# Up-projections of a two-layer encoder: half the row tiles by a 2x2 scheme of seven products

## The chip, the cores and the metric

The kernel runs on one core of a Trainium2 chip. The metric is device time in microseconds: the time of one execution, taken as the median of several runs. TensorE (PE in the profile) multiplies matrices from SBUF into PSUM, VectorE (DVE) and ScalarE (ACT) do elementwise work on both memories, GpSimd (POOL) does little here, and SyncE (SP) issues most transfers from HBM. Each engine works through its own queue in order; semaphores make one wait for another.

## The reference

256 tokens of width 2048 pass two layers, one with attention and pooling, one with an mLSTM. Both layers end in the same gated MLP, the part that matters here:

```
def conv_ffn(x, w_up, conv_w, conv_b, w_down):
    u = x @ w_up
    up = jnp.pad(u, ((0, 0), (1, 1), (0, 0)))
    c = conv_w.astype(u.dtype)
    u = c[0] * up[:, :-2] + c[1] * up[:, 1:-1] + c[2] * up[:, 2:] + conv_b.astype(u.dtype)
    gate, val = jnp.split(u, 2, axis=-1)
    return (jax.nn.silu(gate) * val) @ w_down
```

`w_up` is 2048 x 11264 (gate and value, 5632 columns each), `w_down` 5632 x 2048, everything float32. `x` has gone through an RMS norm before, and the result is added to the residual.

## The kernel before

**Precision.** Each float32 operand is split into a high part in a shorter matmul format (float32r) and a low part, the rest. A product is then three matmuls: high by high, high by low, low by high. Activations are split once (`norm.xx`, 16 K tiles x {high, low} x 256 tokens). Weights are split as they stream in.

**The stream of weights.** `Stream` holds one list of weight chunks of 128 x 1024 float32 (512 KB) in the order in which TensorE uses them. `load` issues a chunk's transfer on SP into a raw buffer `w` (six of them); `split` makes the high part on ScalarE (L89) and the low part on VectorE (L90) in a buffer `hl` (four). `next` hands TensorE its chunk and first tops up both, five chunks loaded ahead and two split ahead. The hosts' part (`_up_chunks`, `_down_chunks`, `_ffn_order`) only lays the weights out in that order.

**The MLP.** The 44 row tiles of the hidden width (128 gate rows and 128 value rows each) are done in chunks of 4, 8, 8, 8, 8 and 8 (`FCH`). For each chunk, `up` makes its row tiles, and then `down` adds the previous chunk's share to the residual, 512 output columns at a time (four groups); the last chunk's `down` ends the layer.

- `up` (L886) runs `stat_group`: 16 K tiles, weights stationary, tokens moving. Per K tile there are two matmuls 512 columns wide (the weights' high part by both parts of the activations) and two 256 wide (low part by high). The result lies in PSUM with hidden rows on partitions. `gather` (L365 to L368) adds its two halves with a ScalarE copy and a VectorE add, L890 multiplies by the norm's scale `R` per token, L894 to L897 are the convolution over tokens, L900 to L903 the gate and the split of the result into `g`.
- `down` (L933) runs `mov_part`: activations stationary, 512 weight columns moving, six matmuls per K tile, then two VectorE adds into `x` (`residual`, L376).

**PSUM.** Both kinds of group use tag `mm`, two buffers of two banks each: one is filled while the other is read. The remaining four banks are the tag `ps`, for transposes and small products.

**Order.** TensorE's order is the program's order (a manual schedule). The other engines' queues are ordered by the compiler's scheduler. `Weave` keeps small side tasks (norms, attention heads) that TensorE takes in between: `wv.tick(dt)` advances a nominal clock after each few matmuls, and a task is continued when its delay has passed.

Of the kernel before, what the change touches and what calls it, by code (L numbers as in the profile page):

```python
# [9 lines left out]
F32 = mybir.dt.float32  # L10
# [6 lines left out]
P = 128  # L17
# [47 lines left out]
class Stream:  # L65


    def __init__(self, nc, wpool, spool, srcs, load_ahead, split_ahead):
        self.nc, self.wpool, self.spool, self.srcs = nc, wpool, spool, srcs
        self.la, self.sa = load_ahead, split_ahead  # L70
        self.w, self.hl = {}, {}
        self.n_load = self.n_split = self.at = 0

    def load(self, pieces=1):
        i = self.n_load
        width = self.srcs[i].shape[-1]
        n = width // pieces
        w = self.wpool.tile([P, CH * P], F32, tag="w", name=f"w{i}")
        for c in range(0, width, n):
            self.nc.sync.dma_start(w[:, c : c + n], self.srcs[i][:, c : c + n])  # L80
        self.w[i] = w, n, width
        self.n_load += 1

    def split(self, then=None):
        i = self.n_split
        w, n, width = self.w.pop(i)
        hl = self.spool.tile([P, 2, CH * P], F32R, tag="hl", name=f"hl{i}")
        for c in range(0, width, n):
            (self.nc.vector.tensor_copy if i + c == 0 else self.nc.scalar.copy)(hl[:, 0, c : c + n], w[:, c : c + n])  # L89
            self.nc.vector.tensor_sub(hl[:, 1, c : c + n], w[:, c : c + n], hl[:, 0, c : c + n].bitcast(F32))  # L90
            then and then(c // n)
        self.hl[i] = hl
        self.n_split += 1
# [63 lines left out]
def trunk(ctx: ExitStack, tc: tile.TileContext, gx, xT, xn, call, catt, cml, weights, out):  # L157
# [212 lines left out]
    def bc(ap, n):  # L370
        return ap.unsqueeze(1).to_broadcast([ap.shape[0], n, ap.shape[1]])
# [500 lines left out]
    def ffn_layer(layer, norm, nxt):  # L872
        with ExitStack() as es:
            def lp(name, bufs):
                return es.enter_context(tc.tile_pool(name=name, bufs=bufs, reuse_waits="tile"))

            tp = lp(f"ff{layer}", 2)

            def cw(tl, j):
# [5 lines left out]

            def up(f, gt, i):  # L886
                ps = stat_group(xx, list(range(KT)), f"up{layer}_{f}")
                wv.until(lambda: norm.R is not None)
                u = gather(tp, ps, f"up{layer}_{f}")
                v.tensor_mul(u, u, bc(norm.R, 2))  # L890
                y = tp.tile([P, 2, S], F32, tag="y", name=f"y{layer}_{f}")
                for j in range(2):
                    tl = f + j * FT
                    a.activation(y[:, j, :], u[:, j, :], AF.Identity, scale=cw(tl, 1), bias=cw(tl, 3))  # L894
                    v.scalar_tensor_tensor(y[:, j, 1:S], u[:, j, 0 : S - 1], cw(tl, 0), y[:, j, 1:S],  # L895
                                           ALU.mult, ALU.add)
                    v.scalar_tensor_tensor(y[:, j, 0 : S - 1], u[:, j, 1:S], cw(tl, 2), y[:, j, 0 : S - 1],  # L897
                                           ALU.mult, ALU.add)
                s_ = tp.tile([P, S], F32, tag="silu", name=f"s{layer}_{f}")
                a.activation(s_, y[:, 0, :], AF.Silu)  # L900
                v.tensor_mul(s_, s_, y[:, 1, :])
                a.copy(gt[:, i, 0, :], s_)
                v.tensor_sub(gt[:, i, 1, :], s_, gt[:, i, 0, :].bitcast(F32))  # L903

            def down_end(gt, b, kts):
# [26 lines left out]

            def down(c, gt, last):  # L933
                kts = list(range(FCH[c]))
                for b in range(NB):
                    if last and nxt is None and b == NB - 1:
                        down_end(gt, b, kts)
                        break
                    ps = mmp.tile([P, 2, 512], F32, tag="mm", name=f"dn{layer}_{c}_{b}")
                    mov_part(ps, lambda k: gt[:, k], kts, True, True)  # L940
                    residual(ps, b)
                    if last and nxt is None:
                        nc.sync.dma_start(out[:, :, b * 512 : b * 512 + 512], x[:, :, b * 512 : b * 512 + 512])
                    elif last:
                        nxt.add(b)

            wv.add(norm.finish(), 4.0)
            f, gts = 0, []
            for c, n in enumerate(FCH):
                gt = actp.tile([P, 8, 2, S], F32R, tag=f"B{c % 2}", name=f"g{layer}_{c}")  # L950
                gts.append(gt)
                for i in range(n):
                    up(f, gt, i)
                    f += 1
                if c:
                    down(c - 1, gts[c - 1], False)
            down(len(FCH) - 1, gts[-1], True)

# [68 lines left out]

def _ffn_order():

    seq, u, d = [], 0, 0  # L1030
    for c, n in enumerate(FCH):
        seq += [("u", u + i) for i in range(4 * n)]
        u += 4 * n
        if c:
            m = FCH[c - 1] // 4 * 8
            seq += [("d", d + i) for i in range(m)]
            d += m
    m = FCH[-1] // 4 * 8
    seq += [("d", d + i) for i in range(m)]
    return seq  # L1040
# [100 lines left out]
```

## Time and profile before

| | before |
|---|---|
| median of 3 runs | 2205.43 us (2205.32 to 2205.55) |
| span of the profiled execution | 2203.1 us |
| granted TensorE clock | 1.000 |
| bytes read from HBM | 411.58 MB, 188 GB/s over the span |

The profiled execution's span runs from the first to the last instruction; the time of a run also holds the start and the end around it. In the page, a group of instructions shows its line, engine, operation, output and inputs by the program's names, shapes and count, then busy time, the mean of one in ns, and the idle time of the engine just in front with what ended most of it. Matmuls are pipelined, so the sum of single durations is more than the time they take; the chain that ended last (the work followed back from the last instruction) gives pieces that add up to the span.

### The profile page before, as it was taken

To read this page: it belongs to the slowest core of one execution; us is meant where nothing else is said; L and a number is where in the kernel's file an instruction comes from. 1 tells how busy PE (TensorE), PEld (TensorE's weight loads), DVE (VectorE), ACT (ScalarE), POOL (GpSimd) and SP (SyncE) were. 2 spreads that over 40 slices of the span, in tenths; PEclk is the share of its full clock that TensorE was granted. 3 is DMA by queue.
4 is the path that set the end of the run, shared out by engine and by line. 5 is a ranking of instruction groups with operands and counts; after the bars stand their busy time and mean duration, and the time that the engine had idled before them with its cause. 6 is when DMAs were issued, how large, how long until landed. Compare 5 with 4: busy or idle time off the path is not lost.

```text
span 2203.1 us, 30458 instructions
## 1 busy us (share of the span) xinstructions
PE 2197.9 (100%) x11616; PEld 1883.7 (86%) x11616; DVE 1525.5 (69%) x2172; ACT 1169.0 (53%) x1664; POOL 28.1 (1%) x40
## 2 busy tenths in 40 slices
PE   9999999999999999999999999999999999999999
PEld 8888888888888888889888888888888888888887
DVE  7686677776776767666767676667777677676764
ACT  7665555554554545456555454555555455454542
POOL 0020000000000000000000000000000000000000
PEclk9999999999999999999999999999999999999999
DMA  9555556556565666656565555556555656555664
GB/s 323 179 164 170 175 191 187 190 189 198 184 194 188 192 191 191 196 171 205 162 202 177 185 181 171 186 177 191 186 191 189 197 185 193 189 191 191 192 191 144
DMA packets 118036, 415.71 MB, mean 189 GB/s; under 512 B 13082, under 2 KB 15426, under 8 KB 117890
## 3 DMA queue, kind: packets, MB, share of 16 engines
q1 hardware_dynamic: 114656, 409.76, 58.2%
q10 hardware_dynamic: 3074, 3.75, 0.6%
q8 instruction: 91, 1.49, 0.3%
q14 instruction: 55, 0.45, 0.1%
q0 software_dynamic: 160, 0.26, 0.0%
HBM read 411.58 MB, written 2.14 MB: 188 GB/s over the span
## 4 chain that ended last, share of the span: by engine, by line
PE 100%; DVE 0%; issue 0%
PE up L203 45%; PE dn L203 21%; PE op L203 8%; PE mv L203 4%; PE mq L203 4%; PE mk L203 4%; PE mo L203 4%; PE qproj L203 3%; PE pool L203 1%; PE kproj L203 1%; PE vproj L203 1%; PE qk L203 1%; PE av L203 1%; PE end L203 0%; PE xt L254 0%; PE sc L203 0%
## 5 line engine op out<-in xcount | busy, mean ns | idle before, releaser
L90 DVE TENSOR_TENSOR hl<-w,hl 128x1024 fp32r<-128x1024 f32 (+2 forms) x772 | 939.1, 1218 | 466.6 <-ACT hl L89 464.8
L89 ACT CAST hl<-w 128x1024 fp32r<-128x1024 f32 (+1 forms) x771 | 806.9, 1047 | 677.3 <-PE dn L203 242.1
L203 PE MATMUL up<-xx,hl 128*128 128x512 f32 (+1 forms) x5632 | 984.2, 337 | 0.0
L203 PEld LDWEIGHTS up<-xx,hl 128*128 128x128 f32 x5632 | 857.9, 188 | 125.9
L203 PE MATMUL dn<-hl,g 128*128 128x512 f32 x2064 | 471.3, 389 | 0.0
L203 PEld LDWEIGHTS dn<-hl,g 128*128 128x128 f32 x2064 | 386.2, 188 | 79.5
L366 ACT COPY tb_up<-up 128x512 f32<-128x512 f32 x88 | 51.7, 587 | 154.0 <-PE up L203 154.0
L367 DVE TENSOR_TENSOR tb_up<-up,tb_up 128x512 f32<-128x512 f32 x88 | 60.8, 691 | 97.0 <-ACT tb_up L366 97.0
L894 ACT ACTIVATE y<-tb_up,cst 128x256 f32<-128x256 f32 x176 | 96.4, 595 | 47.0 <-DVE tb_up L890 47.0
L203 PE MATMUL mk<-xx,hl 128*128 128x512 f32 (+1 forms) x512 | 92.2, 337 | 0.0
L203 PE MATMUL mq<-xx,hl 128*128 128x512 f32 (+1 forms) x512 | 92.1, 337 | 0.0
L203 PE MATMUL mv<-hl,xx 128*128 128x512 f32 (+2 forms) x480 | 91.7, 350 | 0.0
L203 PE MATMUL op<-hl,cat 128*128 128x512 f32 x384 | 91.6, 393 | 0.0
L203 PE MATMUL mo<-hl,xx 128*128 128x512 f32 x384 | 90.4, 391 | 0.0
L203 PE MATMUL op<-hl,mcat 128*128 128x512 f32 x384 | 89.5, 392 | 0.0
L203 PEld LDWEIGHTS mq<-xx,hl 128*128 128x128 f32 x512 | 79.2, 188 | 11.6
L203 PEld LDWEIGHTS mk<-xx,hl 128*128 128x128 f32 x512 | 79.0, 188 | 11.4
L203 PEld LDWEIGHTS mv<-hl,xx 128*128 128x128 f32 x480 | 78.3, 189 | 11.2
L203 PEld LDWEIGHTS op<-hl,mcat 128*128 128x128 f32 x384 | 71.5, 188 | 14.6
L203 PEld LDWEIGHTS mo<-hl,xx 128*128 128x128 f32 x384 | 71.0, 188 | 14.2
L203 PEld LDWEIGHTS op<-hl,cat 128*128 128x128 f32 x384 | 70.9, 188 | 14.1
L895 DVE SCALAR_TENSOR_TENSOR y<-tb_up,cst,y 128x255 f32<-128x255 f32 x176 | 76.8, 478 | 0.0
(209 smaller groups left out, 1270.4 us busy)
## 6 DMA issues: line engine op xcount, KB each, us to landing
w<-in_up SPq DMA_DIRECT2D x352, 512.0 KB, 3.6
w<-in_dn SPq DMA_DIRECT2D x176, 512.0 KB, 4.1
w<-in_m_in SPq DMA_DIRECT2D x124, 512.0 KB, 4.1
w<-in_a_in SPq DMA_DIRECT2D x46, 512.0 KB, 4.4
w<-in_a_out SPq DMA_DIRECT2D x32, 512.0 KB, 3.4
w<-in_m_out SPq DMA_DIRECT2D x32, 512.0 KB, 3.5
w<-in_m_g SPq DMA_DIRECT2D x5, 432.0 KB, 3.4
x<-in_xn SPq DMA_DIRECT2D x4, 512.0 KB, 9.5
```

What stands on the lines that cost most here:

```text
L89: (self.nc.vector.tensor_copy if i + c == 0 else self.nc.scalar.copy)(hl[:, 0, c : c + n], w[:, c : c + n])
L90: self.nc.vector.tensor_sub(hl[:, 1, c : c + n], w[:, c : c + n], hl[:, 0, c : c + n].bitcast(F32))
L203: pe.matmul(out_, lhsT, rhs, start=start, stop=stop, skip_group_check=True)
L366: a.copy(tb, ps[:, :, 1, :])
L367: v.tensor_add(tb, ps[:, :, 0, :], tb)
L894: a.activation(y[:, j, :], u[:, j, :], AF.Identity, scale=cw(tl, 1), bias=cw(tl, 3))
L895: v.scalar_tensor_tensor(y[:, j, 1:S], u[:, j, 0 : S - 1], cw(tl, 0), y[:, j, 1:S], ALU.mult, ALU.add)
```

## The change

In each layer's chunks 2 to 6, the last four of the eight row tiles are no longer made by `up` but by `quads`, one "quad" per chunk. The first four, and all of the first chunk, stay as they are.

**The scheme.** A quad's product is (256 tokens x 2048) by (2048 x 1024). The tokens are cut in two blocks of 128, K in pairs of 128, the columns in two halves of 512. Seven block products, in Winograd's form of Strassen's scheme, take the place of eight. Each product has tokens stationary, 512 columns moving, and three matmuls per K pair. The operands are blocks or sums of blocks:

- sums of activations (`sums`, four of them, `sx`) are made once per layer on VectorE and split by ScalarE and VectorE; they use a buffer of the next chunk's `g` as scratch;
- sums of weights (four blocks, two per chunk): the stream's chunk 2 of each K pair is loaded as two copies of block 12, then chunk 1's content (blocks 11 and 22) is added to it by a second, accumulating transfer on GpSimd's queue; chunk 3 (blocks 22 and 21) has two VectorE adds before its split. So a K pair takes three chunks, and four more chunks per quad carry block 21 for the seventh product: 28 chunks where four row tiles took 16.

**PSUM.** Products 1 and 3 accumulate over the whole quad in one `mm` buffer, products 5, 7, 6, 4 in the four `ps` banks. The 28 quad steps (six matmuls each) are spread between the slots of the other groups by `_ffn_plan`: `up` and `down` are generators now and yield between chunks. The first quad starts with chunk 2's first slot, the next three at slot 8 of 32, the last from slot 6 to 24, with the block-21 steps behind.

**After the products.** `decode` combines the seven with six VectorE and some ScalarE operations and applies the norm's scale per token (a partition here). `finish` transposes the results on TensorE (four 128 x 128 per row tile), copies them out, and goes on in `tail`, the old end of `up`.

**Buffers.** In the MLP the stream has seven raw and five split buffers, seven loads and three splits ahead; `tail` writes the gate over `y` and has no buffer of its own for it.

The core of the diff:

```diff
     def load(self, pieces=1):
         i = self.n_load
-        width = self.srcs[i].shape[-1]
+        src = self.srcs[i]
+        kind, src, plus = src if isinstance(src, tuple) else ("plain", src, None)
+        width = src.shape[-1]
...
+        if plus is not None:
+            self.nc.gpsimd.dma_start(w[:, :width], plus, accum_op=ALU.add)
...
+        if kind == "one":
+            self.one = w
+        if kind == "two":
+            self.nc.vector.tensor_add(w[:, 0:512], w[:, 0:512], self.one[:, 0:512])
+            self.nc.vector.tensor_add(w[:, 512:1024], w[:, 512:1024], w[:, 0:512])
...
+            def sums():
+                vv = actp.tile([P, 2, KT // 2, S], F32, tag="B1", name=f"v{layer}")
+                for h in range(2):
+                    ks = slice(8 * h, 8 * h + 8)
+                    v.tensor_add(vv[:, 0], norm.xx[:, ks, 0, :].bitcast(F32), norm.xx[:, ks, 1, :].bitcast(F32))
...
+                    v.tensor_sub(s1, a21, a22)
+                    v.tensor_add(s3, a11, a21)
+                    yield 3.0
+                    v.scalar_tensor_tensor(s2, s1, -1.0, a11, ALU.mult, ALU.subtract)
+                    v.tensor_sub(s4, s3, a12)
+                    v.tensor_sub(s4, s4, a22)
...
+                    for j in range(4):
+                        hi, lo = (sx[:, j, 4 * h : 4 * h + 4, i, :] for i in range(2))
+                        a.copy(hi, raw[:, j])
+                        v.tensor_sub(lo, raw[:, j], hi.bitcast(F32))
+                        yield 2.0
...
+            def product(bank, act, w, c, first, last):
+                (xh, xl), (wh, wl) = act, (w[:, j, c : c + 512] for j in range(2))
+                mm(bank, xh, wh, first, False)
+                mm(bank, xh, wl, False, False)
+                mm(bank, xl, wh, False, last)
+                wv.tick(0.68)
...
+            def quads(fs, gt, i0, name):
+                banks = {}
+                m = KT // 2
+                for p in range(m):
+                    ends = p == 0, p == m - 1
+                    for k in range(3):
+                        hl = st.next()
...
+                        left = ((1, block_of(2 * p, 0)), (3, sum_of(3, p))), \
+                            ((5, sum_of(0, p)), (7, sum_of(2, p))), ((6, sum_of(1, p)), (4, block_of(2 * p + 1, 1)))
+                        for n, (j, act) in enumerate(left[k]):
+                            product(banks[j], act, hl, n * 512, *ends)
+                        if p == m - 1 and k == 0:
+                            c12 = cp1.tile([P, 512], F32, tag="c12", name=f"c12_{name}")
+                            a.copy(c12, banks[1])
+                        if p == m - 1 and k == 2:
+                            c12, c21, c22 = decode(banks, c12, name)
+                            wv.add(finish(c12, c22, fs[2:], gt, i0 + 2, name), 7.0)
+                        yield
+                for p in range(0, m, 2):
+                    hl = st.next()
+                    for n in range(2):
+                        product(banks[1], block_of(2 * (p + n) + 1, 0), hl, n * 512, False, p + n == m - 1)
+                    if p == m - 2:
+                        c11 = cp1.tile([P, 512], F32, tag="c11", name=f"c11_{name}")
+                        a.activation(c11, banks[1], AF.Copy, scale=norm.rcol[:, 0:1])
+                        wv.add(finish(c11, c21, fs[:2], gt, i0, name), 4.0)
+                    yield
+            def decode(banks, c12, name):
...
+                v.tensor_add(c12, c12, banks[6])
+                v.tensor_add(c21, c12, banks[7])
+                a.activation(c21, c21, AF.Copy, scale=r1)
+                a.activation(c12, c12, AF.Copy, scale=n0)
+                v.scalar_tensor_tensor(c12, banks[3], n0, c12, ALU.mult, ALU.add)
+                v.scalar_tensor_tensor(c12, banks[5], n0, c12, ALU.mult, ALU.add)
+                v.scalar_tensor_tensor(c22, banks[5], r1, c21, ALU.mult, ALU.add)
+                v.scalar_tensor_tensor(c21, banks[4], r1, c21, ALU.mult, ALU.subtract)
+                return c12, c21, c22
+            def finish(top, bottom, fs, gt, i0, name):
+                for n, f in enumerate(fs):
+                    tr = psp.tile([P, 2, S], F32, tag="ps", name=f"tr{layer}_{f}")
+                    for j in range(2):
+                        for t, src in enumerate((top, bottom)):
+                            c = (2 * j + n) * P
+                            pe.transpose(tr[:, j, t * P : t * P + P], src[:, c : c + P], ident)
+                    u = tp.tile([P, 2, S], F32, tag="tb", name=f"tb_{layer}_{f}")
+                    a.copy(u, tr)
+                    tail(u, f, gt, i0 + n)
+                    yield 2.5
...
+            wv.add(sums_ready(), 8.0)
+            st.la, st.sa, st.more = 7, 3, (lp(f"fw{layer}", 1), lp(f"fh{layer}", 1), st.at + len(_ffn_plan()))
...
+def _ffn_plan():
+    plan = []
     for c, n in enumerate(FCH):
+        whole = n - 4 if c else n
+        fill = [("n", c, i) for i in range(whole)]
+        if c:
+            down = [("d", c - 1, b) for b in range(NB)]
+            fill = fill[:2] + down[:1] + fill[2:3] + down[1:2] + fill[3:] + down[2:]
+        slots = []
+        for e in fill:
+            slots += [e] * (4 if e[0] == "n" else FCH[e[1]] // 2)
...
+        if c > 1:
+            for k in range(4):
+                here[k + 1].append(("s", c - 1, 0))
+        first, end = (0, len(slots)) if c == 1 else (8, len(slots)) if not late else (6, 24)
+        for k in range(3 * m):
+            here[first + k * (end - first) // (3 * m)].append(("s", c, 0))
+        if late:
+            for k in range(4):
+                here[end + k].append(("s", c, 0))
+        for e, extra in zip(slots, here):
+            plan += [e] + extra
```

In a plan, "n" is one chunk of an up group, "d" one of a down group, "s" one quad step.

More of the change, by code (lines that the diff above doesn't have):

```diff
@@ L959, in trunk @@
+            for e in run.values():
+                assert next(e, None) is None
+            st.la, st.sa, st.more = 5, 2, None
     norms = [Norm(0), None]
```

165 lines of the change are left out of this document (120 added, 45 removed).

## The prediction

> **What bounds the kernel now.** I read the page's head and chain first, to see which engine ends the program.
>
> ```profile
> span 2203.1 us, 30458 instructions
> PE 2197.9 (100%) x11616; PEld 1883.7 (86%) x11616; DVE 1525.5 (69%) x2172; ACT 1169.0 (53%) x1664; POOL 28.1 (1%) x40
> ...
> PE 100%; DVE 0%; issue 0%
> ```
>
> TensorE never waits: 100% of the span and of the chain. Matmuls taken off it shorten the program as long as everything else keeps its cover; DVE at 69% is the nearest cover. Busy times of single matmuls overlap, so I take their price from the chain in order of time, where the pieces add up.
>
> ```profile
> 256.15 3.48 PE up L203 x20
> 260.06 0.71 PE up L203 x4
> ...
> 413.01 89.16 PE up L203 x512
> 502.18 43.53 PE dn L203 x192
> ```
>
> Eight up-projection tiles (64 matmuls each, half of them 512 and half 256 columns wide) take 89.16 us, 11.145 us a tile. A down-projection matmul (512 columns, a new stationary block each time) takes 43.53/192 = 0.2267 us. Between the first two pieces lies 260.06 − 256.15 − 3.48 = 0.43 us, and this piece of the timeline fills it:
>
> ```profile
> 259.46 0.60 PE L254 MATMUL xt<-cst,x 128*128 128x128 f32 x4
> ```
>
> four transposes, 0.1075 us each on the path.
>
> **The matmuls removed and added.** A "quad" is four row tiles of one chunk (1024 columns of the weights, gate and value). Before: 4 × 11.145 = 44.58 us. After: seven products × eight K pairs × three matmuls = 168, all 512 wide with a new stationary block each, the form of the down row: 168 × 0.2267 = 38.09 us. That is −6.49 us, and with five quads a layer and two layers −64.9 us. The results come out with tokens on partitions, so `finish` transposes them back, 16 per quad, 160 × 0.1075 = +17.2 us. On TensorE alone: −47.7 us.
>
> **The wait that the change can add.** The `mm` tag has two buffers, and a group's end is read while the next group fills the other. During a quad products 1 and 3 hold one (`two`), so consecutive up and down groups share the other. What lies between is one quad step of six matmuls, 6 × 0.2267 = 1.36 us. The reading takes this long now:
>
> ```profile
> 634.71 2.67 PE L203 MATMUL dn<-hl,g 128*128 128x512 f32 x11
> 634.91 0.59 ACT L366 COPY tb_up<-up 128x512 f32<-128x512 f32 x1 [1.74 <-PE up L203]
> ...
> 635.53 0.69 DVE L367 TENSOR_TENSOR tb_up<-up,tb_up 128x512 f32<-128x512 f32 x1 [1.10 <-ACT tb_up L366]
> ```
> ```profile
> 678.24 2.01 PE L203 MATMUL up<-xx,hl 128*128 128x512 f32 x10
> ...
> 678.44 1.29 DVE L376 TENSOR_TENSOR x<-x,dn 128x512 f32<-128x512 f32 x2 [0.41 <-PE dn L203]
> ```
>
> From the switch to the next group until the buffer is read: 635.53 + 0.69 − 634.71 = 1.51 us for an up group, 678.44 + 1.29 − 678.24 = 1.49 us for a down group. The gap from one to the next instruction in these rows (635.53 − 634.91 − 0.59) is 0.03 us, so the buffer is free at about 1.55 us, 0.19 us after the six matmuls end. In the plan I count 36 such ends a layer (9 around the second chunk's quad, 7 in each of the next three, 6 in the last), 72 in all. At the lower bound, ScalarE and VectorE both idle as in these rows (1.74, 1.10 and 0.41 us of idleness in front), 72 × 0.19 = 13.7 us. At the upper bound a whole split has just begun ahead of the eviction: 0.19 + 1.22 (the split's row, below), 101 us. I take 0.35 us, nearer to the lower end: VectorE will seldom be idle (next part), but the splits run up to three chunks ahead of TensorE, and their order is laid out in advance so that evictions can come first. That is +25 us. What queues behind a TensorE that waits is everything: its order is written by hand.
>
> By the Trainium skill, "Perfetto Trace Analysis", section Matmuls, independent groups should rotate through different PSUM banks so that an eviction overlaps the next group's matmuls; that rule speaks against giving one of the two buffers away. Taken alone it would charge the whole 1.55 us at each end, 112 us, and 2205.4 − 47.7 + 112 = 2270 us. The rows speak for less, because the quad steps in between write other banks and are that overlap; no run so far shows it.
>
> **VectorE's load.** A steady pair of an up chunk and a down chunk, by its groups and its window:
>
> ```profile
> L90 DVE TENSOR_TENSOR hl<-w,hl 128x1024 fp32r<-128x1024 f32 x48 | 58.6, 1222 | 30.8 <-ACT hl L89 30.8
> L89 ACT CAST hl<-w 128x1024 fp32r<-128x1024 f32 x48 | 50.4, 1050 | 43.7 <-PE dn L203 23.6 <-PE up L203 20.1
> ...
> L895 DVE SCALAR_TENSOR_TENSOR y<-tb_up,cst,y 128x255 f32<-128x255 f32 x16 | 7.0, 478 | 0.0
> L897 DVE SCALAR_TENSOR_TENSOR y<-tb_up,cst,y 128x255 f32<-128x255 f32 x16 | 7.0, 477 | 0.0
> L890 DVE TENSOR_TENSOR tb_up<-tb_up,R 128x512 f32<-128x512 f32 x8 | 5.5, 692 | 0.3
> L367 DVE TENSOR_TENSOR tb_up<-up,tb_up 128x512 f32<-128x512 f32 x8 | 5.5, 691 | 8.8 <-ACT tb_up L366 8.8
> ```
> ```profile
> L376 DVE TENSOR_TENSOR x<-x,dn 128x512 f32<-128x512 f32 x94 | 60.4, 684 | 18.6 <-PE dn L203 18.6
> ...
> L903 DVE TENSOR_TENSOR g<-s,g 128x256 fp32r<-128x256 f32 x88 | 36.8, 419 | 0.0
> L901 DVE TENSOR_TENSOR s<-s,y 128x256 f32<-128x256 f32 x88 | 36.8, 418 | 0.6 <-ACT s L900 0.6
> ...
> L740 DVE SCALAR_TENSOR_TENSOR tb_k<-tb_k,R 128x512 f32<-128x512 f32 x8 | 5.5, 692 | 0.3
> ...
> L427 DVE TENSOR_TENSOR rot_k<-rot_k,qt_k 128x512 f32<-128x512 f32 x2 | 1.3, 683 | 0.0
> ```
> ```profile
> 413.01:545.71 132.70, 132.70 (x706) 113.85 (x705) 91.23 (x120) 68.04 (x88) 0.00 (x0) 1.00 0.60 191
> 0.00:30.00 30.00, 28.77 (x116) 23.61 (x117) 21.80 (x41) 20.81 (x37) 0.71 (x9) 1.00 0.97 376
> ```
>
> In the window rows the fields after the length are PE, PEld, DVE, ACT and POOL, then clock, DMA share and GB/s. A tile's tail on VectorE is 0.69 + 0.69 + 4 × 0.478 + 0.418 + 0.419 = 4.13 us. Now: 48 splits (58.6) + 8 tails (33.0) + 8 residual adds (5.5) = 97.1 us of durations in 132.7; the window says 91.2, because neighbours overlap by some 6%.
>
> After, in the same stretch: a quad has 28 weight chunks where four tiles had 16, so 60 splits × 1.222 = 73.3; the two sums that stay on VectorE, 16 adds × 0.683 (the L427 row) = 10.9; four tails × 4.13 = 16.5; four tails without the two 0.69 us steps, 2.75 × 4 = 11.0; `decode`, six operations × 0.69 (the L740 row) = 4.1; residuals 5.5. Sum 121.3 us. TensorE's own time there is 44.58 + 43.53 + 38.09 + 1.72 = 127.9 us. So VectorE goes from 73% to 95% by durations, or 89% with the 6% overlap. It does not become the bound by load alone, and I charge nothing beyond the eviction wait above; its cover is 127.9 − 114 = 14 us of slack a chunk. ScalarE gains 12 casts × 1.05 = 12.6 us on 68.0: no bound.
>
> `sums` adds per layer and half one 2048-wide add (twice the 1.222 row, 2.4), five 512-wide operations and four subtractions (9 × 0.69): 8.6 us, 17 us a layer, from the moment the norm's scale is there. The first chunk's 44.6 us of TensorE time hides the first half; the second half falls beside the first quad, which needs it only from its fifth K pair, twelve quad steps later. Hidden; without cover it costs 2 × 17 = 34 us.
>
> **Decode to transpose.** `finish` is put 7.0 us behind the last product, and TensorE must then wait for `c12` and `c22`: 0.2 us, two adds, two ScalarE steps (0.59 each), three more VectorE operations, about 0.2 + 1.38 + 1.18 + 2.07 = 4.8 us. In time if nothing comes between; with three splits woven in (3.7 us) 8.5 us, 1.5 us late. Bounds 0 and 15 us over ten quads; I take +5.
>
> **DMA.** The densest quad stretch of a middle chunk is 24 slots (four down groups, two up groups: 43.53 + 22.29 us) and 24 quad steps (32.65 us), 98.5 us. It loads 48 × 0.524 MB = 25.2 MB, and eight accumulating transfers bring 4.2 MB more: 298 GB/s if those cost like loads. The opening 30 us ran at 376 GB/s, so there is room. The trace has no accumulating transfer:
>
> ```profile
> w<-in_up SPq DMA_DIRECT2D x352, 512.0 KB, 3.6
> ...
> R<-rr POOLq DMA_DIRECT2D x2, 128.0 KB, 6.4
> ```
>
> From below it is a plain load; from above I have only that POOL's queue took 6.4 us for a quarter of the bytes. A summed chunk then needs 3.6 + 6.4 = 10 us or more; seven raw buffers at 127.9/60 = 2.13 us a chunk give 14.9 us, so I charge 0. POOL holds nothing else in that stretch (0.00 busy); behind its waits stands only the power of the next norm, after the last quad. SP issues 120 more loads and waits for nothing but a free raw buffer, which a summed chunk keeps until the next chunk's adds have read it.
>
> By the Trainium skill, "Collectives: The Full Stack", section The bandwidth ceiling, an add in the DMA path reads two sources and so runs at half the rate of a copy. Then the stretch would ask for 341 GB/s, still under 376, and the sum stays; no run here shows it yet.
>
> **Sum.** −64.9 + 17.2 + 25 + 5 = −17.7 us. The profiled execution's span is 2203.1 us, 2.3 us under the runs' 2205.4, start and end that do not change. 2205.4 − 17.7 = 2187.7, **2188 us**.
>
> **Rivals.**
>
> *The waits stay at their floor or vanish.* 2205.4 − 47.7 = 2158 with no wait, 2171 with 13.7 us of them. For it: the evictions now find both engines idle. Against: VectorE's idle share falls from 31% to about 11%.
>
> *VectorE sets the pace (slower).* Its queue is strictly in order, so idle time in front of a late input is lost. Place: the ten quad chunks. Break-even: 132.7 − 121.3 = 11.4 us of idleness a chunk, where the chunk now has 132.7 − 91.2 = 41.5. If each of eight tails still waits for ScalarE as in the L367 row (8.8 us in all), each down group 0.41 us (1.6), and of the 30.8 us behind casts 4.8 stay, it is 15.2 us: 136.5 us a chunk, +3.8, ten times +38, 2243 us. Against: the waits behind casts are there because TensorE frees buffers no faster; with a fifth `hl` buffer they should go first, and durations overlap by 6%.
>
> *Accumulating DMA saturates the queues (slower).* Capacity of the 98.5 us stretch is 37.0 MB; loads leave 11.8, so from 2.8 times a load's price DMA sets the pace. At four times: 42 MB, 111.7 us, +13.2 − 4.8 gained, ten times: 2289 us. Against: nothing in the trace is that dear.
>
> **Chances.** Forecast, 2172 to 2204: 0.45. Floor, 2158 to 2172: 0.17. VectorE's pace: 0.28. DMA: 0.10. About 0.2% (4.4 us) is what a measurement of this kernel tells from no change. Faster: 0.17 plus most of 0.45, 0.58; same 0.07; slower 0.35. The range runs from 2160, nearly no waits, to 2240, just short of VectorE's priced case, so that about 0.18 stays outside; the likeliest case alone has 2172 to 2204.
>
> **What would show it.** In the chain of waits, quad pieces at 0.227 us a matmul and about 38 us a quad show the count right. Idle TensorE of some 30 us, released by the up and down evictions and by `c12`/`c22`, shows the waits right; over 48 us makes the forecast's sign wrong. VectorE near 90% in a middle chunk with TensorE still at 97% or more shows load right; VectorE at 97% with TensorE waiting for `hl` is the second rival. Splits that wait for `w` from the summed load are the third.

## The result, and the profile after

The changed kernel takes 2545.85 us (median of four, 2531.02 to 2551.76) where the kernel before, run beside it, takes 2205.45: 1.1533 times as long, interval 1.1499 to 1.1568. I had forecast 2188 us and a range up to 2240. The profiled execution spans 2549.6 us, 346.5 more than before.

The head of the page after, and its row for the new add of weights; in a row of groups the fields are form and count, then busy us and mean ns, then the idle time of the engine ahead of it and what ended it:

```profile
span 2549.6 us, 30255 instructions
...
PE 2264.8 (89%) x10896; PEld 1873.6 (73%) x10896; DVE 1759.2 (69%) x2474; ACT 1316.0 (52%) x1840; POOL 97.9 (4%) x120
...
q1 hardware_dynamic: 131936, 472.68, 55.9%
q0 software_dynamic: 11680, 42.21, 9.3%
...
L102 DVE TENSOR_TENSOR w<-w,w 128x512 f32<-128x512 f32 x80 | 55.4, 692 | 415.0 <-DMA w<-in_qm 415.0
...
w<-in_qm SPq DMA_DIRECT2D x240, 512.0 KB, 5.1
...
w<-in_qm POOLq DMA_DIRECT2D x80, 512.0 KB, 8.0
```

TensorE went from 100% to 89%, and of the others only GpSimd, which issues the new transfers, is fuller than before in share, at 4%: VectorE stands at 69% in both. So no engine's load is the bound; something waits. The row L102 says what: VectorE stood still for 415 us, 5.2 us in the mean in front of each of its 80 adds, until the transfer behind the operand had landed. The accumulating transfer lands 8.0 us after its issue (median, last row, POOL's queue), a plain load of the same size 5.1.

TensorE's waits in the trace after (who waits, for whom, us in total, times, longest):

```profile
PE dn L219 <- DVE tb_up L383: 124.3, 17, 10.8
PE up L219 <- DVE x L392: 31.0, 11, 5.2
PE p L219 <- DVE tb_up L383: 23.2, 6, 4.6
PE npr L219 <- DVE n L1085: 21.3, 2, 10.7
...
PE p L219 <- DVE hl L106: 17.9, 15, 2.1
```

TensorE seldom waits for the weights themselves: with the last row, all rows with `hl` make 36.0 us. For evictions of the `mm` buffers (L383 and L392) it waits 208.3 us, up to 10.8 us at a time for an operation of 0.7. How one is late, from the timelines of five engines over the same 20 us: VectorE, then the issues on SP and POOL, then ScalarE and TensorE:

```profile
841.90 0.69 DVE L102 TENSOR_TENSOR w<-w,w 128x512 f32<-128x512 f32 x1 [7.25 <-DMA w<-in_qm]
...
843.24 6.89 DVE L106 TENSOR_TENSOR hl<-w,hl 128x1024 fp32r<-128x1024 f32 x6
859.27 0.69 DVE L102 TENSOR_TENSOR w<-w,w 128x512 f32<-128x512 f32 x1 [9.14 <-DMA w<-in_qm]
859.88 0.68 DVE L383 TENSOR_TENSOR tb_up<-up,tb_up 128x512 f32<-128x512 f32 x1
```
```profile
845.62 0.33 SPq L89 DMA_DIRECT2D w<-in_qm  x1
```
```profile
832.66 0.86 POOL L91 DMA_DIRECT2D w<-in_qm  x1 [18.18 <-DVE x L392]
851.37 0.86 POOL L91 DMA_DIRECT2D w<-in_qm  x1 [17.85 <-DMA w<-in_dn]
868.98 0.86 POOL L91 DMA_DIRECT2D w<-in_qm  x1 [16.74 <-DVE y L911]
```
```profile
848.77 0.59 ACT L382 COPY tb_up<-up 128x512 f32<-128x512 f32 x1 [1.74 <-PE up L219]
```
```profile
848.57 1.55 PE L219 MATMUL p<-hl,sx 128*128 128x512 f32 x6
860.62 5.15 PE L219 MATMUL dn<-hl,g 128*128 128x512 f32 x12 [10.50 <-DVE tb_up L383]
```

An add ends at 842.6 and six splits in a row follow, which free raw buffers. The plain load of the next summed chunk goes out at 845.62. The accumulating transfer may start only when that has landed, at 851.37. It lands 7.8 us later, and the next add begins at 859.27. All that time the add stands at the head of VectorE's queue, and right behind it stands the eviction L383, whose ScalarE half was done at 849.36 (its row is in the next to last fence). TensorE's next group needs that buffer: 10.50 us. So the loop closes: the split behind the add frees the buffer of the next load. The accumulations come 18.7 and 17.6 us apart, where a K pair of a middle chunk should take 98.5/8 = 12.3 us.

Behind the wait TensorE is also slow: twelve matmuls in 5.15 us, which take 2.9 in full flow. The windows around it (length, then PE, PEld, DVE, ACT and POOL busy, clock, DMA share, GB/s):

```profile
840.00:860.00 20.00, 9.60 (x49) 7.57 (x47) 8.92 (x10) 6.50 (x7) 0.86 (x1) 0.88 0.63 197
860.00:870.00 10.00, 9.38 (x31) 7.51 (x32) 8.28 (x12) 3.52 (x6) 0.86 (x1) 0.74 0.40 122
870.00:880.00 10.00, 9.59 (x42) 7.51 (x40) 5.67 (x8) 5.92 (x7) 0.00 (x0) 1.00 0.86 250
```

The granted clock is 0.74 in the ten us behind the wait and 1.00 in the next ten; over the whole span it is 0.951, before 1.000. All of TensorE's idle time is 280.9 us (before 1.2), so of the 346.5 us 279.7 are idleness and 66.8 longer work, although 47.7 us of work were taken off.

### The profile page after: what moved, and what is told of

Same layout as the page of the kernel before. It is cut to its first block, busy times and chain, and to the rows that moved or that the text cites. A ratio compares the mean times of both kernels' runs of the same rounds, so it can differ in the third digit from the quotient of the medians.

```text
span 2549.6 us, 30255 instructions
## 1 busy us (share of the span) xinstructions
PE 2264.8 (89%) x10896; PEld 1873.6 (73%) x10896; DVE 1759.2 (69%) x2474; ACT 1316.0 (52%) x1840; POOL 97.9 (4%) x120
## 3 DMA queue, kind: packets, MB, share of 16 engines
q1 hardware_dynamic: 131936, 472.68, 55.9%
q0 software_dynamic: 11680, 42.21, 9.3%
## 5 line engine op out<-in xcount | busy, mean ns | idle before, releaser
L105 ACT CAST hl<-w 128x1024 fp32r<-128x1024 f32 (+2 forms) x891 | 923.9, 1046 | 732.3 <-PE dn L219 141.7
L106 DVE TENSOR_TENSOR hl<-w,hl 128x1024 fp32r<-128x1024 f32 (+2 forms) x892 | 1068.8, 1217 | 259.3 <-ACT hl L105 256.4
L219 PE MATMUL dn<-hl,g 128*128 128x512 f32 x2064 | 547.6, 418 | 153.4 <-DVE tb_up L383 124.3
L219 PE MATMUL up<-xx,hl 128*128 128x512 f32 (+1 forms) x3072 | 589.9, 347 | 54.0 <-DVE x L392 31.0
L219 PEld LDWEIGHTS up<-xx,hl 128*128 128x128 f32 x3072 | 503.7, 195 | 150.6 <-issue 32.0
L102 DVE TENSOR_TENSOR w<-w,w 128x512 f32<-128x512 f32 x80 | 55.4, 692 | 415.0 <-DMA w<-in_qm 415.0
L219 PE MATMUL p<-hl,sx 128*128 128x512 f32 x960 | 264.3, 399 | 0.0
L219 PE MATMUL p<-hl,xx 128*128 128x512 f32 x720 | 210.2, 405 | 50.9 <-DVE tb_up L383 23.2
L219 PEld LDWEIGHTS p<-hl,sx 128*128 128x128 f32 x960 | 179.1, 192 | 36.3
L219 PEld LDWEIGHTS p<-hl,xx 128*128 128x128 f32 x720 | 130.7, 192 | 84.5 <-issue 25.6
L91 POOL DMA_DIRECT2D w<-in_qm x80 | 68.6, 857 | 1515.7 <-DVE hl L106 278.5
```

The costliest lines, as they stand in the source:

```text
L91: self.nc.gpsimd.dma_start(w[:, :width], plus, accum_op=ALU.add)
L102: self.nc.vector.tensor_add(w[:, 0:512], w[:, 0:512], self.one[:, 0:512])
L219: pe.matmul(out_, lhsT, rhs, start=start, stop=stop, skip_group_check=True)
```

## The experiments

Times below are medians against the kernel before, run on the same chip. The letters in the expectations stand for theories; the text or the expectation names each. Kernels ran on several chips, but the kernel before took 2205.45 to 2205.59 us on all of them, so I compare their times directly. Kernels that leave the accumulating transfers out miss sums, and those with shared banks mix products; except where I call one complete, their results are not the reference's, and they are there for their times.

**The accumulating transfer left out.** Theory A: VectorE's queue is held by the add that waits for it. The four products with `two` or `one` in them have a wrong operand for it.

```
-        if plus is not None:
-            self.nc.gpsimd.dma_start(w[:, :width], plus, accum_op=ALU.add)
```

> Leaves out the accumulating transfers (two of the four weight sums are not formed, so the quads' results are not those of the reference); all else as in the changed kernel. Theory A (latency: the add of the third chunk, 5.2 us of waiting 80 times, stands in VectorE's ordered queue until the accumulation has landed, and everything queues behind it): the wait before that add falls from 415 us to under 40 us, a K pair takes 12.3 to 13.5 us instead of 17.7, and the time is 2170 to 2215 us. Theory B (VectorE's load and the shared PSUM buffer in the quad stretches): little changes, over 2450 us. Theory C (the bytes of the accumulating transfers saturate DMA): as A, 2170 to 2215 us; this run does not tell A from C.

Measured 2282.3 us, ratio 1.0348 (1.0333 to 1.0364). 264 of the 340 us go with the transfer, as A and C both say; the runs with the pinned add and with the early chunk tell them apart. But 2282 is well above A's range, and still 77 above before; the wait in front of the add is 55.8 us, now for plain loads, where A had under 40. TensorE idles 83.4 us in this kernel. An eviction in its VectorE timeline, then its ScalarE half and the TensorE row that waits for it:

```profile
586.57 1.23 DVE L104 TENSOR_TENSOR hl<-w,hl 128x1024 fp32r<-128x1024 f32 x1 [0.44 <-ACT hl L103]
587.71 0.88 DVE L907 SCALAR_TENSOR_TENSOR y<-tb,cst,y 128x255 f32<-128x255 f32 x2
...
590.87 1.23 DVE L104 TENSOR_TENSOR hl<-w,hl 128x1024 fp32r<-128x1024 f32 x1
592.01 0.43 DVE L913 TENSOR_TENSOR y<-y 128x256 f32<-128x256 f32 x1
592.34 0.69 DVE L381 TENSOR_TENSOR tb_up<-up,tb_up 128x512 f32<-128x512 f32 x1
```
```profile
590.30 0.57 ACT L380 COPY tb_up<-up 128x512 f32<-128x512 f32 x1
```
```profile
593.18 0.93 PE L217 MATMUL p<-hl,xx 128*128 128x512 f32 x3 [2.90 <-DVE tb_up L381]
```

Here no transfer is late. From 586.57 on VectorE is not idle, and the eviction simply stands behind the tails of two row tiles and a split. ScalarE's half is late as well: it starts at 590.30, when TensorE has just stopped (593.18 − 2.90), behind steps of the same tails.

**The activation sums pinned.** In the same kernel as above the scheduler may no longer move the first add of `sums` forward: its place on VectorE is the one it has in the program. Theory D: where it had been put, among the small steps of the norm, it delays the first matmul of the MLP.

```
-                    v.tensor_add(vv[:, 0], norm.xx[:, ks, 0, :].bitcast(F32), norm.xx[:, ks, 1, :].bitcast(F32))
+                    tc.keep_in_program_order(v.tensor_add(
+                        vv[:, 0], norm.xx[:, ks, 0, :].bitcast(F32), norm.xx[:, ks, 1, :].bitcast(F32)))
```

> As the run without accumulating transfers (which leaves out two of the four weight sums), and the first operation of the activation sums is pinned behind all that stands before it on VectorE, the norm's chain with it. Theory D (the scheduler put the sums between the small steps of the norm's scale, so that TensorE waits 10.7 us for it at the start of each MLP): the two waits of 10.7 us go, and with the slow clock behind them some 5 us more, 2250 to 2262 us against 2282. If the scale is late for another reason: no change.

2264.12 us, 1.0264 (1.0249 to 1.0279): 18.2 less, 2 us above D's range, and the row `npr` is gone from the waits. To see `sums` alone, a kernel with the quads taken out (every row tile goes by the eight products, no summed chunk is loaded) and the sums left where the scheduler puts them. All four sums are on VectorE; the expectation is wrong in giving two to GpSimd, whose 40 instructions are those of before. This kernel is complete, and the change's order of groups and its buffers stay too:

```
-        whole = n - 4 if c else n
+        whole = n
...
+        plan += slots
+        continue
```

> All row tiles go by the eight products of before, no summed chunk is loaded, added to or multiplied; what stays of the change are the activation sums on VectorE (two) and GpSimd (two), not pinned, with nothing that reads them. If they are hidden, as I predicted: 2203 to 2208. If, where the scheduler puts them among the norm's small steps, they hold TensorE's first matmul of an MLP back as they do in the changed kernel (twice 10.7 us, and the clock behind it), 2225 to 2235.

2235.41 us, 1.0136 (1.0120 to 1.0151). Sums that nothing reads cost 29.9 us, with that order and those buffers. The VectorE timeline of that kernel shows how, at the start of an MLP; then TensorE's:

```profile
267.82 0.15 DVE L228 TENSOR_TENSOR re_n<-ry_n 128x2 f32<-128x2 f32 x1
...
270.62 0.15 DVE L229 TENSOR_TENSOR re_n<-re_n,rv_n 128x2 f32<-128x2 f32 x1
270.69 2.29 DVE L935 TENSOR_TENSOR v<-xx 128x2048 f32<-128x2048 f32 x1
...
276.44 0.15 DVE L1085 TENSOR_SCALAR n<-re_n 128x1 f32<-128x1 f32 x1
```
```profile
276.67 1.19 PE L219 MATMUL npr<-dg,cst 128*128 128x256 f32 x2 [10.66 <-DVE n L1085]
277.30 7.95 PE L219 MATMUL up<-xx,hl 128*128 128x512 f32 x32
```

The norm's Newton steps are 0.15 us each, but between them VectorE does the sums, the 2048-wide add of 2.29 us included. TensorE waits 10.66 us, and the 32 matmuls behind it, which take 32 × 0.174 = 5.6 us in the flow before, take 7.95. Twice 10.66 and twice 2.4 are 26 of the 30 us; the other 4 I can't assign.

**The add of weights pinned.** Is the add early because the scheduler put it there, taking the accumulation for faster than it is (A1), or is the data so late that it holds the quads wherever it stands (A2)? Accumulating transfers and all results stay; L102 is pinned to its place in the program, as are the activation sums.

```
-            self.nc.vector.tensor_add(w[:, 0:512], w[:, 0:512], self.one[:, 0:512])
+            self.pin(self.nc.vector.tensor_add(w[:, 0:512], w[:, 0:512], self.one[:, 0:512]))
```

> The changed kernel with complete results and accumulating transfers; the add that waits for the accumulated chunk and the activation sums are pinned behind all that stands before them on VectorE. Theory A1 (the scheduler took the accumulation as landed sooner and floated the add ahead of evictions and splits): the wait before the add falls from 415 us to under 150 us and the time from 2546 to 2300 to 2400 us. Theory A2 (the raw buffers alone limit it: the chunk cannot be loaded earlier wherever the add stands): 2450 us or more.

2287.93 us, 1.0381 (1.0362 to 1.0401), a little under A1's range: 258 of the 340 us come back with the order alone. The two pins were not tried apart here; in the kernels without accumulation the sums' pin was worth 18.2. The row of the add in this kernel, and its windows beside those of the changed kernel (second fence, same stretch):

```profile
L102 DVE TENSOR_TENSOR w<-w,w 128x512 f32<-128x512 f32 x80 | 54.8, 686 | 0.0
...
400.00:700.00 300.00, 292.13 (x1413) 239.59 (x1414) 253.84 (x332) 185.17 (x237) 14.61 (x17) 1.00 0.82 261
```
```profile
400.00:700.00 300.00, 250.92 (x1160) 204.19 (x1161) 208.93 (x281) 151.75 (x197) 12.02 (x14) 0.93 0.71 214
```

VectorE's idle time in front of the 80 adds is 0.0 us, the DMA engines move 261 GB/s instead of 214, and TensorE is busy 292 of 300 us instead of 251. The transfers do keep pace, and the order is what cost (A1). It is the best complete version that I found with quads, and still slower than before.

**The summed chunk a K pair earlier.** Theory C: the bytes of the accumulating transfers saturate the queues (my third rival). Same transfers, but the summed chunk has two raw buffers of its own and is loaded one K pair ahead; there are four split buffers for five. The adds are not pinned.

```
+        if self.kind(i) == "one":
+            j = next((j for j in range(i + 1, len(self.srcs)) if self.kind(j) == "one"), None)
+            if j is not None and self.more is not None and j < self.more[2]:
+                self.fetch(j, 1)
...
+        home = self.more[0] if kind == "one" else self.wpool
```

> Same transfers, bytes and sums as the changed kernel, but the chunk that is accumulated is loaded and summed one K pair (some 12 to 17 us) earlier, in two raw buffers of its own beside six for the others; for the space the fifth split buffer goes, and splits run two chunks ahead instead of three. Theory A: the wait before the third chunk's add falls from 415 us to under 80 us and the time to 2190 to 2270 us. Theory C: the traffic is the same, so 2450 to 2560 us. Theory B: no better than the changed kernel, 2530 us or more, since one split buffer is gone.

2326.63 us, 1.0555 (1.0537 to 1.0573). The same bytes in 219 us less: 254 GB/s and a DMA share of 0.84 between 400 and 700 us, where the changed kernel had 214 and 0.71. Bytes were not what held it, and C is out. A's direction is right and its range too low: the wait in front of the add is still 101.8 us, where A had under 80.

**What holds the rest.** From the kernel without accumulation and with pinned sums (2264.1), two costs taken away one at a time and then together. First the `mm` buffer that products 1 and 3 take from the groups: instead products 3 and 7 share one `ps` bank and 6 and 4 another, so the evicted sums are wrong.

```
-                                two = mmp.tile([P, 2, 512], F32, tag="mm", name=f"p13_{name}")
-                                banks[1], banks[3] = two[:, 0], two[:, 1]
...
+                                banks[(7, 4)[k - 1]] = banks[(3, 6)[k - 1]]
```

> As the run with pinned sums and without accumulating transfers, and products 1 and 3 take no mm buffer: products 3 and 7 share one ps bank, 6 and 4 another, so that their values mix and the quads' results are not the reference's, while the matmuls, their count and every other step stay. Theory E (the waits at group ends come from the one buffer left): TensorE's waits for the up and down evictions, some 60 us of idleness in the run without accumulation, fall under 15 us, and the time is 2190 to 2220 us. Theory F (VectorE's load starves TensorE of split weights): within 15 us of the run with pinned sums.

2225.01 us, 1.0086 (1.0071 to 1.0101): 39.1 less, 5 us over E's range. The two largest of TensorE's waits with the buffer shared (2264.1), then without:

```profile
PE p L217 <- DVE tb_up L381: 15.8, 8, 2.8
PE dn L217 <- DVE tb_up L381: 15.1, 14, 1.7
```
```profile
PE dn L217 <- ACT g L914: 18.9, 8, 7.3
PE dn L217 <- DVE g L915: 11.5, 8, 2.0
```

Every wait for an eviction is gone (51.4 us over the rows with `tb_up` and `x`), but the down groups now wait 30.4 us for `g`, a wait that no row has with the buffer shared. So 39.1 is a difference of the two. Then the two adds of weights on VectorE left out, the buffer shared again:

```
-        if kind == "two":
-            self.nc.vector.tensor_add(w[:, 0:512], w[:, 0:512], self.one[:, 0:512])
-            self.nc.vector.tensor_add(w[:, 512:1024], w[:, 512:1024], w[:, 0:512])
```

> As the run with pinned sums and without accumulating transfers, and the two remaining weight sums are left out as well (no weight sums at all, the quads' results are not the reference's): VectorE has 10.9 us a chunk less, 110 us in all, and no instruction of its own waits for a transfer. Theory F: 2200 to 2235 us. Theory E: the shared buffer still makes its waits, but evictions find a freer VectorE; 2230 to 2255 us.

2233.7 us, 1.0127 (1.0112 to 1.0142): 30.4 less, inside both ranges, so this run alone does not tell E from F. And both:

> Leaves out the accumulating transfers and the two vector adds of the weight sums (so four of the seven products have a wrong operand) and gives products 1 and 3 no buffer of their own (they share the banks of products 7 and 4, so the evicted sums are wrong); the activation sums stay pinned. Against 2264.1 us with the pinned sums alone, the shared buffer was worth 39.1 us and the vector adds 30.4 us, each alone. Theory E (each is a separate queue behind VectorE, the two add up): 2264.1 - 39.1 - 30.4 = 2195, idle TensorE below 20 us. Theory F (both hold the same waits, an eviction that comes late, so that with one gone the other costs little): 2210 to 2225, no lower than the better of the two alone by more than 15 us. If 2175 or less, the product matmuls' own pace isn't the loss that I took it for.

2200.8 us, 0.9978 (0.9967 to 0.9989): 63.3 less, nearly the sum of the two (69.5), and 24.2 below the better one alone, where F allowed 15. Theory E holds, the two costs are nearly separate. With no accumulation, no adds and no shared buffer, and so with wrong results, the kernel is 4.7 us faster than before. TensorE's waits in that kernel, and some pieces of its chain of waits:

```profile
PE dn L214 <- DVE g L912: 11.1, 6, 2.1
PE tr L1023 <- DVE c L1011: 3.7, 2, 1.9
...
PE tr L1023 <- DVE c L1012: 0.7, 2, 0.3
```
```profile
474.16 1.40 PE p L214 x6
475.56 2.74 PE dn L214 x12
```

A product step of six takes 1.37 to 1.40 us there, and over the trace, outside the stretches at half clock, a product matmul takes 0.232 us from start to start and a down matmul 0.231 (0.227 before). The clock is 0.994: seven stretches of 3.4 us at half clock.

**More cover at the group ends.** From the version with both pinned (2287.9): the quads' steps are dealt out so that two of them, not one, stand behind the last chunk of every group.

```
-        for k in range(3 * m):
-            here[first + k * (end - first) // (3 * m)].append(("s", c, 0))
+        for j in range(first, end):
+            ends = j + 1 == len(slots) or slots[j + 1] != slots[j]
...
+            n = 1 + ends - (near and not late) + (late and j == first)
+            here[j] += [("s", c, 0)] * n
```

> The version with both the accumulated add and the activation sums pinned (2287.9 us), with the quads' steps dealt out otherwise: two steps of products stand behind the last slot of each group instead of one, so 12 matmuls (2.7 us) instead of 6 (1.4 us) lie between the last matmul into the shared buffer and the next group's first. If the group ends' waits are the reason for most idle TensorE time (theory G), half of the 39 us that the shared buffer is worth comes back or more: 2250 to 2272. If VectorE's load in a chunk sets it (theory H), the cover only moves the wait: 2280 to 2295.

2352.61 us, 1.0675 (1.0657 to 1.0693): 65 us slower, which neither theory had. The three largest of TensorE's waits in this kernel, then ScalarE's timeline at one of them:

```profile
PE p L220 <- ACT hl L105: 60.6, 16, 10.1
PE up L220 <- DVE x L393: 16.5, 9, 4.8
PE p L220 <- DVE c L1015: 14.5, 5, 5.5
```
```profile
627.01 3.89 ACT L105 CAST hl<-w 128x1024 fp32r<-128x1024 f32 x4 [1.82 <-DVE w L103]
```

TensorE idles 122.6 us where the version it was made from idles 76.1. Most of the growth is the first row: 60.6 us of products that wait for the cast of a split chunk, 24.5 before. ScalarE's cast in turn waits for the second weight add, as the timeline shows. My reading, not tested, is that two steps in a row use up split chunks faster than they are made, so that cover at the group ends is bought with cover for the weights. The groups behind `x` wait no less (16.5 us, 9.2 before). Whether cover alone would help stays open.

**Other places for the weight sums.** All four on VectorE, with no accumulating transfer and complete results:

```
+            self.nc.vector.tensor_add(w, w, self.zero)
```

> No accumulating transfers: the two sums are made on VectorE as well, by one more add of 128x1024 per K pair (1.22 us, 80 times, 98 us in all); the result is complete. Theory A: VectorE's durations in a middle chunk are 121.3 + 9.8 = 131 us against 128 us of TensorE, about 123 us with the 6% overlap, so VectorE is the bound or close to it: 2200 to 2270 us. Theory B: more load on the engine that bounds, over 2600 us. Theory C: as A.

2347.35 us, 1.0643 (1.0628 to 1.0659): above A's range and far under B's, and 65 us more than the same kernel without these adds (2282.3), for 98 us of VectorE's time. All four on GpSimd, again complete:

```
+            self.nc.gpsimd.tensor_add(w, w, self.zero)
...
+            self.nc.gpsimd.tensor_add(w[:, 0:512], w[:, 0:512], self.one[:, 0:512])
+            self.nc.gpsimd.tensor_add(w[:, 512:1024], w[:, 512:1024], w[:, 0:512])
```

> All four weight sums on GpSimd, as elementwise adds between loaded chunks, none by DMA and none on VectorE; the result is complete. GpSimd's two-input rows of 128x256 took 0.84 to 1.21 us, so one add of 1024 columns and two of 512 are 6.8 to 9.7 us per K pair (an estimate by length), under the 12.3 us of TensorE. Theory A: the wait moves to a shorter chain off VectorE's queue, 2180 to 2240 us. Theory B: VectorE loses 11 us a chunk, some gain but over 2400 us. Theory C: as A. If GpSimd and VectorE hinder each other, splits (1.22 us now) get longer and the time is over 2250 us.

2375.46 us, 1.0764 (1.0748 to 1.0780), although GpSimd has little else to do: outside A's and B's ranges, and where the last sentence puts it (over 2250). Groups of this kernel from 300 to 1000 us, and the same split where no such add runs (the first experiment):

```profile
L107 DVE TENSOR_TENSOR hl<-w,hl 128x1024 fp32r<-128x1024 f32 x288 | 426.6, 1504 | 68.3 <-ACT hl L106 66.8
...
L93 POOL TENSOR_TENSOR w<-w,w 128x1024 f32<-128x1024 f32 x40 | 119.9, 2997 | 371.0 <-DMA w<-in_qm 286.6 <-DVE hl L107 36.3 <-DVE y L910 28.0
```
```profile
L104 DVE TENSOR_TENSOR hl<-w,hl 128x1024 fp32r<-128x1024 f32 x304 | 369.2, 1223 | 80.2 <-ACT hl L103 78.1
```

The mean split takes 1.50 us instead of 1.22. In the whole trace the 635 splits that overlap no GpSimd add take 1.22 us in the mean, the 81 that lie wholly within adds 1.90. So the load that left VectorE came back as slower work, and more of it: with 160 adds less VectorE is busy 1931.7 us, in the first experiment 1771.4.

## Why the prediction was wrong, by its own steps

Where the 388 us between the floor that I named (2158) and the measurement (2546) lie, by the runs:

| taken away | us |
|---|---|
| order of the weight adds and the activation sums (pinned) | 257.9 |
| the accumulating transfers, with the sums pinned (and the pin of the add with them) | 23.8 |
| shared `mm` buffer and the two weight adds (39.1 and 30.4 alone) | 63.3 |
| what stays over 2158 | 42.8 |

**The step that failed is DMA, "so I charge 0".** I compared a rate with a rate: a summed chunk needs 10 us or more, seven raw buffers give 14.9. Both were of the right size (845.62 to 859.27 is 13.65 us). Yet the term that I put at 0 was worth 264 us, by the first experiment. What I did not do was follow the add, which the change puts on VectorE with a wait of its own: which instructions stand behind it in that strict queue, and who waits for them. With 13.65 us of latency, an add placed a few us too early blocks the evictions and the very splits that free the next buffer. It was the third rival's sign ("splits that wait for `w`") with another mechanism: not bytes, as the early load and the pinned add show at 254 and 261 GB/s with the same bytes. My 2289 for that rival had the right direction for the wrong reason. That the order on VectorE is what costs is shown; that the scheduler counted the accumulation as fast is my reading of why it chose that order, and was not tried.

**`sums`, "Hidden".** It is hidden from TensorE's matmuls, but not from the norm's chain, which runs on the same engine at the same moment: 29.9 us alone. That this is near the 34 that I gave for no cover is chance: the 34 added up VectorE's own durations, the 29.9 are mostly TensorE's wait behind the norm. I looked for the first reader of its result, not for what it displaces.

**VectorE's load, "I charge nothing beyond the eviction wait".** The load was estimated nearly rightly: 250 of 300 us busy in the pinned kernel without accumulation, 83% where I gave 89%. But the two adds, 160 × 0.69 = 110 us of VectorE time, cost 30.4. So the slack that I counted did not hide them from a TensorE that waits for one instruction in that queue. This is the second rival's reason, and its 2243 stands nearer to the 2264 without accumulation than my own sum; but its sign, a TensorE that waits for `hl`, has no row there, as the waits are for evictions.

**The group ends, +25.** The mechanism was right, and the shared buffer is worth 39.1 us, within 13.7 to 101, but the term was too small. In the kernel without accumulation and with pinned sums, TensorE idles 35.6 us for evictions in front of up and down groups, 0.49 us an end over the 72 ends where I took 0.35. At these ends the product matmul just ahead also lasts longer: of 268 places in front of an up or down matmul, it takes over 0.3 us at 72 with the buffer shared and at 4 without, some 11 us in all. The 15.8 us in front of a quad's first product, which needs an `mm` buffer itself, I had not counted. That the net is 39.1 comes from the 30.4 us that the down groups wait for `g` once the buffer is given back; what sets that wait I did not follow. The Trainium skill, "Perfetto Trace Analysis", section Matmuls, asks for groups that rotate through different PSUM banks. The 112 us that I worked out for that rule taken alone were too much, but it pointed the right way: the shared buffer's 39.1 us are over a third of the 106 by which the kernel without accumulation lies above the floor.

**Decode to transpose, +5.** 4.4 us with everything else taken out (the `tr` rows). In the kernels that share the buffer no `tr` waits; there products wait 8.8 us for `c`, in the changed kernel too. The size was right, the place only without the shared buffer.

**The matmuls, −64.9 + 17.2.** Count and kind were right. A product matmul takes 0.232 us, not 0.2267: some 8 us in all.

**What I had no term for: the clock.** I took each wait at its own length. Behind a wait of some us the clock halves for a while: 0.951 over the changed kernel, 2549.6 × 0.049 = 125 us, part of it in the idle time itself. Even in the kernel with all three taken away, seven half-clock stretches of 3.4 us are 12 of its 43 us over the floor; 15.9 are idleness that before had not, the products' pace is some 8, and down matmuls at 0.231 us instead of 0.227 another 8. These counts overlap a little, and why the down matmuls are slower is not shown.

## What to carry to other kernels

A new instruction that waits for a transfer costs what stands behind it in its engine's queue, not its own duration: follow that queue to whoever waits for it, and fix the instruction's place if a scheduler chooses it. Work put into an engine's slack is free only if nothing urgent passes through that engine: here a quad saves 4.8 us of TensorE, and a single late eviction cost it up to 10.8. Price a stall of a full TensorE above its length: here the 279.7 us of idleness came with 66.8 us of longer work, although 47.7 were taken off.

## What the runs showed of the hardware

An accumulating transfer of 512 KB from HBM took 8.0 us from issue to landing (7.1 with the adds pinned), a plain one in the same kernel 5.1. In the DMA engines' time the accumulating queue took 9.3% of the span for 42.21 MB, 0.22% a MB, the plain one 55.9% for 472.68 MB, 0.118% a MB: 1.9 times as dear a byte. No plain transfer of this size ran on GpSimd's queue, so how much of that is the queue's and not the add's is not shown. The prediction cited half the rate of a copy from the Trainium skill ("Collectives: The Full Stack", section The bandwidth ceiling); the trace agrees with that size. Of my third rival's break-even, 2.8 times, it stays short.

In these traces the granted clock is 1.00 or 0.50 and nothing between, and inside a program every stretch at 0.50 lasts 3.4, 6.8, 10.2 or 13.7 us: 38 of them in the changed kernel. All 38 begin during a wait of TensorE or within 2 us behind it. In the kernel with all three taken away, seven of the eight waits of 1.8 to 2.1 us led to one each; in the changed one, single waits of up to 3.2 us led to none. By the Trainium skill, "TensorE: Matmul & The Clock Gate", Part 1, the array falls to half rate after an idle window of about 3.4 us and returns after a busy one. The two levels and the length agree; that a wait of half that length can be enough the trace shows against it, and what decides which one is not shown here.

GpSimd's adds made VectorE's splits 23% longer in the mean (1223 to 1504 ns), and those wholly within such adds 56% (1221 to 1899 ns). The Trainium skill, "SBUF — State Buffer", section Who interferes with whom, says that a VectorE instruction with two SBUF inputs contends with a GpSimd one that reads SBUF; the split is such a one, and the trace agrees.
